# Reordering the convolution chunks of a hybrid diffusion backbone: vector taps, sigmoid products and modulation matmuls

## The chip, the core and the metric

The kernel runs on one core of a Trainium2 chip. TensorE (PE in the rows) multiplies matrices into PSUM; VectorE (DVE), ScalarE (ACT) and GpSimd (POOL) work element by element; SyncE (SP) issues the transfers, which run on the core's 16 DMA engines. Each engine works through its own queue in order, and semaphores hold an instruction until what it reads is there and what it writes is free. The metric is the device time of one execution in microseconds, as the median of several runs.

## The reference, cut to what matters

Two layers run over 1024 latent and 256 context tokens of width 1024. The change lies in the first layer's Conformer convolution module, a gated linear unit followed by a depthwise convolution of 31 taps, a LayerNorm and a second matmul; and in the modulation vectors, a small matmul of SiLU(c) with a large weight matrix.

```python
sc = jax.nn.silu(c)
mod_lat = (sc @ ada_w[i] + ada_b[i])[:, None, :]
sh1, sc1, g1, sh2, sc2, g2 = jnp.split(mod_lat, 6, axis=-1)

def conformer_conv(h, w_pw1, b_pw1, w_dw, b_dw, ln_g, ln_b, w_pw2, b_pw2):
    u = h @ w_pw1 + b_pw1
    a, g = jnp.split(u, 2, axis=-1)
    v = a * jax.nn.sigmoid(g)
    v = dwconv(v, w_dw, b_dw)          # 31 taps per channel
    v = jax.nn.silu(layernorm(v, ln_g, ln_b))
    return v @ w_pw2 + b_pw2
```

## The kernel before

Channels lie on the 128 partitions, tokens along the free dimension, in three token tiles: 0 and 1 with 512 latent tokens each, 2 with the 256 context tokens. The convolution stage goes over eight chunks c of 128 channels. It is a software pipeline: the loop body for c convolves chunk c while the matmuls of the gated linear unit for chunk c + 1 run (`q` is that next chunk, `q.v` its gated result). All four compute engines have their order written out by hand here: inside `tc.manual_schedule` an instruction stands on its engine's queue where the program names it. SP's queue alone is ordered by the scheduler.

The pieces of the body, with their lines:

- `glu_mm(q, t, half)` (L193): one half, gate (0) or value (1), of token tile t, three groups of eight matmuls, since every product of full precision is made of a high and a low part (`wh`, `wl`, `xh`, `xl`). The results alternate between two PSUM banks (`glu_ps`).
- `glu_gate` (L746, ScalarE) takes the sigmoid of the gate half; `glu_mul` (L751, VectorE) multiplies it with the value half into `v`. `vp.load` (L799, L792) writes a part of `v` to DRAM and reads it back shifted by one token per tap (`vp`, `vpb`), for TensorE.
- The 31 taps of chunk c are divided. Eight go to TensorE in chunks 0 to 5 (16 in chunk 6, 28 in chunk 7): `taps` (L822), small diagonal matmuls into the one PSUM accumulator `cacc`. `NDV`, 13 taps (8 in chunk 6, none in chunk 7), go to VectorE: `dq` (L843), each of which adds one tap into `cacc`, so they start when TensorE is done with it. The rest are made as products on ScalarE (`first`, L838, and `pq`, L848, `pr`, two buffers) and added by GpSimd (L849) in a second accumulator `a`.
- `last()` (L853): three VectorE adds join `cacc` and `a` to `y`. They free `cacc` for the next chunk's matmuls. `ymean` (L862) accumulates the mean of y on TensorE.
- `ada` (L211): the modulation of block 4 + c, eight matmuls in four parts, each of which reads one 512 KB weight tile `raw`. Then comes a copy out of PSUM (L217, ScalarE) and, in the next chunk as `fin`, a transpose and bias (L223, L226, L231). `ld_ada` (L109) issues the load of a part.
- `w_load`, `w_hi` (L914, ScalarE) and `w_lo` (L919, VectorE, `wl`): load and split of the next two weight tiles of the gated linear unit.

All weight tiles go through the same two `raw` buffers, in the order: modulation parts 0 and 1, parts 2 and 3, two weight tiles. A load therefore waits until the tile two places ahead has been read. `run(steps, n)` takes the next n steps of a list:

```python
pq = [lambda j=j: prod(j)() for j in range(npe + ndve + 1, TAPS)]
dq = [lambda j=j: dve(j) for j in range(npe, npe + ndve)]
return [lambda: part(0), lambda: part(1), lambda: part(2), lambda: part(3), evac, finish]
```

Chunk 7 has no next gated linear unit; its body is the `else` branch. There `load_ada` (L878) loads 2 MB modulation weights of the second layer into the input tiles that are no longer needed. Behind the loop come the LayerNorm and the second matmul.

Of the kernel before, what the change touches and what calls it, by code (L numbers as in the profile page):

```python
# [52 lines left out]
def hybrid_dit_kernel(  # L53
# [555 lines left out]
    with ExitStack() as cs:  # L609
# [255 lines left out]
        def run(steps, n):  # L865
            for _ in range(min(n, len(steps))):
                steps.pop(0)()
# [54 lines left out]
        with tc.manual_schedule(engines=CONV_ENGINES):  # L922
# [16 lines left out]
            q = glu_begin(0)  # L939
# [36 lines left out]
            wh = w_hi()  # L976
# [11 lines left out]
            for c in range(KC):  # L988
                wide_taps = M[c] * P > 256
                if wide_taps:  # L990
                    dgs = tap_weights(c)
                r, taps = pe_taps(c, vp, dgs)
                first, pq, dq, last = conv_steps(c, q.v, r, NPE[c], NDV[c])
                ada_ps = pc.tile([P, 512], F32, tag="s", name="ada_ps", bufs=2) if c == KC - 1 else None
                ada = ada_steps(0, 4 + c, lambda u, c=c: araw[c, u], ada_ps)
                if c + 1 < KC:
                    q = glu_begin(c + 1)
                    glu_mm(q, 0, 0)
                    glu_gate(q, 0)
                    glu_mm(q, 0, 1)  # L1000
                    glu_mul(q, 0)
                    if fin:
                        fin()
                    run(taps, 4)
                    run(ada, 2)
                    ld_ada(c, 2)
                    ld_ada(c, 3)
                    first()
                    run(pq, 2)
                    vp = Shifted(c + 1, q.v)  # L1010
                    vp.load(0)
                    if c > 0:
                        ymean(c - 1)
                    glu_mm(q, 1, 0)
                    run(pq, 2)
                    glu_gate(q, 1)
                    run(ada, 2)
                    w_load()
                    w_load()
                    run(dq, 3)  # L1020
                    glu_mm(q, 1, 1)
                    run(ada, 1)
                    run(dq, 3)
                    glu_mul(q, 1)
                    vp.load(1)
                    run(pq, 1)
                    if M[c + 1] * P <= 256:
                        dgs = tap_weights(c + 1)
                    wh = w_hi()
                    glu_mm(q, 2, 0)  # L1030
                    run(dq, 1)
                    w_lo(wh)
                    ld_ada(c + 1, 0)
                    run(pq, 1)
                    glu_gate(q, 2)
                    wh = w_hi()
                    glu_mm(q, 2, 1)
                    run(dq, 1)
                    glu_mul(q, 2)
                    vp.load(2)  # L1040
                    w_lo(wh)
                    ld_ada(c + 1, 1)
                    run(pq, 99)
                    run(dq, 99)
                    fin = ada.pop()
                else:
                    run(ada, 2)
                    ld_ada(c, 2)
                    ld_ada(c, 3)
                    fin()  # L1050
                    first()
                    run(pq, 99)
                    ymean(c - 1)
                    run(taps, 2)
                    run(ada, 3)
                    for i in range(4):
                        load_ada(i)
                    run(taps, 2)
                    run(dq, 99)
                last()  # L1060
        cvs.close()
# [771 lines left out]
```

## Time and profile before

| what | value |
|---|---|
| median of 3 runs | 2767.87 us (2767.05 to 2770.55) |
| the profiled execution | 2768.97 us, its span 2767.2 us |
| TensorE busy over the span | 2646.0 us (96%) |
| VectorE, ScalarE, GpSimd busy | 1622.0, 984.5, 549.5 us |
| mean granted TensorE clock | 0.986 of full speed |
| convolution stage, first to last convolution matmul | 91.6 to about 403 us |

The page's shares are averages over stages with different limits. The stage that the change touches is some 310 us of the 2767. Start and end times below are microseconds from the span's start. "Idle before" is the time for which the engine had nothing to do ahead of a row, with the event that ended it; "issue" there means that the profile shows no event for it.

### The profile page before, as it was taken

How to read it: one execution, taken by the hardware profiler on the slowest of the kernel's cores; microseconds unless marked ns; L12 is line 12 of the kernel's file. 1: busy time of each engine (PE TensorE's matmuls, PEld its weight loads, DVE VectorE, ACT ScalarE, POOL GpSimd, SP SyncE). 2: the span in 40 equal slices, each digit the busy share in tenths (PEclk: the TensorE clock that was granted, in tenths of full speed). 3: DMA queues.
4: the chain of work that ended last, by engine and by line, in shares of the span. 5: the costliest groups of instructions: out<-in, count | busy, mean ns of one | idle time of the engine just before them, and what ended most of it. 6: DMA issues, size and time to landing. Idle time of an engine off the chain costs nothing.

```text
span 2767.2 us, 34117 instructions
## 1 busy us (share of the span) xinstructions
PE 2646.0 (96%) x13860; PEld 2145.8 (78%) x13860; DVE 1622.0 (59%) x2273; ACT 984.5 (36%) x1396; POOL 549.5 (20%) x384
## 2 busy tenths in 40 slices
PE   5999978999999999999999999999999999999997
PEld 3676644778888888888888787788878888888886
DVE  6576635454454544444546757999865545555546
ACT  6444425552211122211123426777652222222223
POOL 1576623230000000000002204566420000000003
PEclk8999999999999999999999999999999999999998
DMA  6554665322111111111111451331111111111111
GB/s 243 163 172 152 203 212 196 109 84 69 39 39 39 38 39 39 39 39 38 37 40 37 152 190 45 73 81 52 39 54 48 52 46 49 51 46 46 53 47 69
DMA packets 81774, 225.38 MB, mean 81 GB/s; under 512 B 10832, under 2 KB 22736, under 8 KB 79312
## 3 DMA queue, kind: packets, MB, share of 16 engines
q1 hardware_dynamic: 81616, 223.20, 24.5%
q8 instruction: 109, 1.79, 0.3%
q14 instruction: 49, 0.40, 0.0%
HBM read 202.00 MB, written 21.16 MB: 81 GB/s over the span
## 4 chain that ended last, share of the span: by engine, by line
PE 78%; DVE 10%; ACT 5%; DMA 3%; issue 2%; POOL 1%; SPq 1%; DVEq 0%; ACTq 0%; POOLq 0%
PE up_ps L193 38%; PE dn_ps L193 18%; PE glu_ps L193 4%; PE wo_ps L193 3%; PE cacc L822 2%; PE pw_ps L193 2%; DVE cacc L843 2%; PE pB L193 2%; DMA raw<-in_adaw_dram 2%; PE pA L193 2%; PE tp L1544 1%; DVE tl L178 1%; PE v_ps L193 1%; PE ada_ps L211 1%; DVE mx L1522 1%
## 5 line engine op out<-in xcount | busy, mean ns | idle before, releaser
L131 DVE TENSOR_TENSOR wl<-raw,wh 128x1024 fp32r<-128x1024 f32 x165 | 204.8, 1242 | 514.7 <-issue 311.1
L193 PE MATMUL up_ps<-x_l,wh 128*128 128x512 f32 (+1 forms) x1760 | 413.8, 369 | 4.2 <-POOL x_l L322 4.2
L193 PE MATMUL up_ps<-x_h,wl 128*128 128x512 f32 (+1 forms) x1760 | 408.7, 368 | 0.2 <-ACT x_h L311 0.2
L193 PE MATMUL up_ps<-x_h,wh 128*128 128x512 f32 (+1 forms) x1760 | 406.9, 368 | 0.0
L193 PEld LDWEIGHTS up_ps<-x_l,wh 128*128 128x128 f32 x1760 | 311.2, 188 | 64.0 <-POOL x_l L322 5.8
L193 PEld LDWEIGHTS up_ps<-x_h,wh 128*128 128x128 f32 x1760 | 310.7, 189 | 55.6 <-issue 0.8
L193 PEld LDWEIGHTS up_ps<-x_h,wl 128*128 128x128 f32 x1760 | 309.9, 189 | 56.0 <-issue 0.8
L257 POOL TENSOR_TENSOR acc<-acc,scrh 128x256 f32<-128x256 f32 (+1 forms) x36 | 37.5, 1041 | 1574.1 <-ACT scrh L256 1572.3
L461 DVE SCALAR_TENSOR_TENSOR y<-dn_ps,mods,y 128x512 f32<-128x512 f32 (+1 forms) x400 | 270.3, 694 | 129.2 <-PE dn_ps L193 129.1
L416 ACT ACTIVATE c<-up_ps,pv 128x1282 f32<-128x1282 f32 (+1 forms) x88 | 115.7, 1316 | 586.8 <-PE up_ps L193 586.8
L129 ACT CAST wh<-raw 128x1024 fp32r<-128x1024 f32 x178 | 185.5, 1043 | 357.7 <-PE dn_ps L193 328.1
L193 PE MATMUL dn_ps<-gl,wh 128*128 128x512 f32 (+1 forms) x800 | 233.0, 372 | 0.7 <-DVE y L461 0.7
L193 PE MATMUL dn_ps<-gh,wl 128*128 128x512 f32 (+1 forms) x800 | 231.5, 371 | 0.0
L193 PE MATMUL dn_ps<-gh,wh 128*128 128x512 f32 (+1 forms) x800 | 231.1, 370 | 0.0
L849 POOL TENSOR_TENSOR a<-a,pr 128x1295 f32<-128x1295 f32 x62 | 190.2, 3068 | 95.8 <-ACT pr L848 93.3
L1538 POOL TENSOR_TENSOR p<-p,rd 128x640 f32<-128x640 f32 (+1 forms) x128 | 154.7, 1240 | 233.0 <-DVE rd L1536 164.5
L420 DVE SCALAR_TENSOR_TENSOR c<-up_ps,pv,c 128x1281 f32<-128x1281 f32 (+1 forms) x88 | 124.6, 1416 | 121.2 <-ACT c L416 121.2
L193 PEld LDWEIGHTS dn_ps<-gl,wh 128*128 128x128 f32 x800 | 142.7, 188 | 31.8 <-DVE y L461 6.4
L193 PEld LDWEIGHTS dn_ps<-gh,wh 128*128 128x128 f32 x800 | 145.1, 188 | 27.0
L193 PEld LDWEIGHTS dn_ps<-gh,wl 128*128 128x128 f32 x800 | 145.1, 188 | 27.0
L843 DVE SCALAR_TENSOR_TENSOR cacc<-v,pv,cacc 128x1295 f32<-128x1295 f32 x86 | 134.9, 1569 | 43.8 <-PE cacc L822 41.7
L424 DVE SCALAR_TENSOR_TENSOR c<-up_ps,pv,c 128x1281 f32<-128x1281 f32 (+1 forms) x88 | 124.5, 1416 | 2.3
(255 smaller groups left out, 4029.0 us busy)
## 6 DMA issues: line engine op xcount, KB each, us to landing
raw<-in_up_dram SPq DMA_DIRECT2D x88, 512.0 KB, 3.4
ada<-in_adaw_dram SPq DMA_DIRECT2D x11, 2048.0 KB, 9.2
raw<-in_down_dram SPq DMA_DIRECT2D x44, 512.0 KB, 3.4
raw<-in_adaw_dram SPq DMA_DIRECT2D x38, 512.0 KB, 4.9
raw<-in_pw_dram SPq DMA_DIRECT2D x32, 512.0 KB, 3.5
vpb<-v_dram SPq DMA_DIRECT2D x32, 256.0 KB, 4.5
qs<-q_dram SPq DMA_DIRECT2D x32, 256.0 KB, 5.9
raw<-in_wo_dram SPq DMA_DIRECT2D x16, 512.0 KB, 3.5
```

The lines of the kernel that those rows point to most:

```text
L129: nc.scalar.copy(out=wh, in_=raw)
L131: lo_engine[0].tensor_sub(out=wl, in0=raw, in1=wh)
L193: nc.tensor.matmul(ps, lhsT=w, rhs=x, start=first and n == 0, stop=last and n == len(seq) - 1)
L257: (eng or nc.gpsimd).tensor_add(out=acc, in0=acc, in1=sq)
L416: nc.scalar.activation(out=c, in_=ps[:, :W], func=AF.Identity, bias=seg("fdb", l * 2 * NJ + ab * NJ + j, 1), scale=wd[1])
L420: nc.vector.scalar_tensor_tensor(out=c[:, 1:W], in0=ps[:, 0:W - 1], scalar=wd[0], in1=c[:, 1:W], op0=ALU.mult, op1=ALU.add)
L424: nc.vector.scalar_tensor_tensor(out=c[:, 0:W - 1], in0=ps[:, 1:W], scalar=wd[2], in1=c[:, 0:W - 1], op0=ALU.mult, op1=ALU.add)
L461: nc.vector.scalar_tensor_tensor(out=h, in0=ps[:, m * n:(m + 1) * n], scalar=mod(l, 5, dc, s), in1=h, op0=ALU.mult, op1=ALU.add)
L822: nc.tensor.matmul(r["acc"][32 * g:32 * g + 32, o:e], lhsT=w[:, (4 * s + g) * 32:(4 * s + g + 1) * 32], rhs=vp.rows(g, s, o, e - o), start ...
L843: nc.vector.scalar_tensor_tensor(out=acc, in0=v[:, j:j + OW], scalar=tap(j), in1=acc, op0=ALU.mult, op1=ALU.add)
L849: return lambda: nc.gpsimd.tensor_tensor(out=r["a2"], in0=r["a2"], in1=pr, op=ALU.add)
L1538: nc.gpsimd.tensor_tensor(out=it.p4[:, hh, :it.wid], in0=it.p4[:, hh, :it.wid], in1=rd[:, hh:hh + 1].to_broadcast([P, it.wid]), op=ALU.mult)
```

## The change

Only the order of calls in the loop body changes. In chunks 0 to 6 parts 0 and 1 of the modulation stand ahead of the convolution matmuls, instead of behind them, and parts 2 and 3 behind `ymean`, instead of between two groups of the gated linear unit. Five products instead of four stand ahead of the second token tile's sigmoid, and a sixth directly behind it. Nine vector taps (all eight in chunk 6) stand ahead of the second token tile's gate product, where six were and a seventh and eighth between later steps. In chunk 7 parts 0 and 1 come behind the first half of the convolution matmuls instead of ahead of the previous chunk's `fin`.

```diff
--- before.py
+++ after.py
@@ -999,34 +999,34 @@
                     glu_gate(q, 0)
                     glu_mm(q, 0, 1)
                     glu_mul(q, 0)
+                    run(ada, 2)
+                    ld_ada(c, 2)
+                    ld_ada(c, 3)
                     if fin:
                         fin()
                     run(taps, 4)
-                    run(ada, 2)
-                    ld_ada(c, 2)
-                    ld_ada(c, 3)
                     first()
-                    run(pq, 2)
+                    run(pq, 3)
                     vp = Shifted(c + 1, q.v)
                     vp.load(0)
                     if c > 0:
                         ymean(c - 1)
-                    glu_mm(q, 1, 0)
-                    run(pq, 2)
-                    glu_gate(q, 1)
                     run(ada, 2)
                     w_load()
                     w_load()
-                    run(dq, 3)
+                    glu_mm(q, 1, 0)
+                    run(ada, 1)
+                    run(pq, 2)
+                    glu_gate(q, 1)
+                    run(pq, 1)
                     glu_mm(q, 1, 1)
-                    run(ada, 1)
-                    run(dq, 3)
+                    run(dq, 9)
                     glu_mul(q, 1)
                     vp.load(1)
+                    wh = w_hi()
                     run(pq, 1)
                     if M[c + 1] * P <= 256:
                         dgs = tap_weights(c + 1)
-                    wh = w_hi()
                     glu_mm(q, 2, 0)
                     run(dq, 1)
                     w_lo(wh)
@@ -1044,18 +1044,18 @@
                     run(dq, 99)
                     fin = ada.pop()
                 else:
-                    run(ada, 2)
-                    ld_ada(c, 2)
-                    ld_ada(c, 3)
                     fin()
                     first()
                     run(pq, 99)
                     ymean(c - 1)
                     run(taps, 2)
+                    run(ada, 2)
+                    ld_ada(c, 2)
+                    ld_ada(c, 3)
+                    run(taps, 2)
                     run(ada, 3)
                     for i in range(4):
                         load_ada(i)
-                    run(taps, 2)
                     run(dq, 99)
                 last()
         cvs.close()
```

VectorE, from the convolution of chunk 1 to the end of its y (`cacc` are the taps, `v<-glu_ps` the gate products, `wl` the weight splits), before:

```order
L843 SCALAR_TENSOR_TENSOR cacc<-v,pv,cacc 128x1295 x6
L751 SCALAR_TENSOR_TENSOR v<-glu_ps,pv,sg 128x512
L843 SCALAR_TENSOR_TENSOR cacc<-v,pv,cacc 128x1295
L919 TENSOR_TENSOR wl<-raw,wh 128x1024
L843 SCALAR_TENSOR_TENSOR cacc<-v,pv,cacc 128x1295
L751 SCALAR_TENSOR_TENSOR v<-glu_ps,pv,sg 128x256
L919 TENSOR_TENSOR wl<-raw,wh 128x1024
L843 SCALAR_TENSOR_TENSOR cacc<-v,pv,cacc 128x1295 x5
L853 TENSOR_TENSOR y_677<-cacc,a_1085 128x512
```

and with the change, in the same place:

```order
L843 SCALAR_TENSOR_TENSOR cacc<-v,pv,cacc 128x1295 x9
L751 SCALAR_TENSOR_TENSOR v<-glu_ps,pv,sg 128x512
L843 SCALAR_TENSOR_TENSOR cacc<-v,pv,cacc 128x1295
L919 TENSOR_TENSOR wl<-raw,wh 128x1024
L843 SCALAR_TENSOR_TENSOR cacc<-v,pv,cacc 128x1295
L751 SCALAR_TENSOR_TENSOR v<-glu_ps,pv,sg 128x256
L919 TENSOR_TENSOR wl<-raw,wh 128x1024
L843 SCALAR_TENSOR_TENSOR cacc<-v,pv,cacc 128x1295 x2
L853 TENSOR_TENSOR y_677<-cacc,a_1085 128x512
```

Three taps went from behind the second split to ahead of the first gate product; the total stays 13.

TensorE from the transpose of the previous modulation block (`ada_pt`) over the convolution matmuls of chunk 1 (`ada_ps` are modulation parts, `xl_470` an input of token tile 1), before:

```order
L223 MATMUL ada_pt<-ident,ada_sb 128x128 x4
L822 MATMUL cacc<-vp,dg 32x512 x8
L822 MATMUL cacc<-vp,dg 32x272 x8
L822 MATMUL cacc<-vpb,dg 32x240 x8
L822 MATMUL cacc<-vpb,dg 32x271 x8
L211 MATMUL ada_ps<-raw,c_80 32x512 x4
L862 MATMUL ymean<-y_677,ones_88 32x512
L862 MATMUL ymean<-y_678,ones_88 32x512
L862 MATMUL ymean<-y_679,ones_88 32x256
L193 MATMUL glu_ps<-xl_470,wh 128x512 x8
```

and with the change:

```order
L211 MATMUL ada_ps<-raw,c_80 32x512 x4
L223 MATMUL ada_pt<-ident,ada_sb 128x128 x4
L822 MATMUL cacc<-vp,dg 32x512 x8
L822 MATMUL cacc<-vp,dg 32x272 x8
L822 MATMUL cacc<-vpb,dg 32x240 x8
L822 MATMUL cacc<-vpb,dg 32x271 x8
L862 MATMUL ymean<-y_677,ones_88 32x512
L862 MATMUL ymean<-y_678,ones_88 32x512
L862 MATMUL ymean<-y_679,ones_88 32x256
L211 MATMUL ada_ps<-raw,c_80 32x512 x4
```

Parts 0 and 1 went from behind the convolution to ahead of it. The row at the end of the second piece is parts 2 and 3, which stood three groups of `glu_ps` further on before.

SP's queue from the write of the first part of a chunk's `v` to the write of its second, before:

```order
L799 DMA v_dram_1093<-v 128x527
L792 DMA vp<-v_dram_1093 128x1x512 x4
L109 DMA raw<-in_adaw_dram 128x1024 x2
L109 DMA raw<-in_pw_dram 128x1024 x2
L799 DMA v_dram_1093<-v 128x527
```

and with the change:

```order
L799 DMA v_dram_1096<-v 128x527
L109 DMA raw<-in_adaw_dram 128x1024 x2
L792 DMA vp<-v_dram_1096 128x1x512 x4
L109 DMA raw<-in_pw_dram 128x1024 x2
L799 DMA v_dram_1096<-v 128x527
```

The loads of modulation parts 2 and 3 changed places with the four shifted copies. Near the end of the loop one 2 MB load (L878) moved too: from behind the last pair of modulation loads to directly ahead of the four shorter `vp` copies for chunk 7.

## Rows read from the trace of the kernel before

**Rows 1.** Chain that ended last, in time; columns: start us, us, what.
```profile
199.40 3.54 DVE wl L919
...
211.12 1.56 issue
```
**Rows 2.** Windows of one chunk: PE, PEld, DVE, ACT, POOL busy; clock, DMA, GB/s.
```profile
239.40:280.50 41.10, 38.27 (x236) 27.32 (x236) 29.09 (x24) 17.70 (x17) 28.45 (x13) 0.96 0.50 159
```
**Rows 3.** Waits, 91.6 to 336.6 us: engine, line, released by; total us, times, longest.
```profile
PE cacc L822 <- issue: 12.2, 5, 2.5
```
**Rows 4.** Timeline of TensorE, one chunk; start us, us, instruction, [idle before].
```profile
212.68 4.54 PE L822 MATMUL cacc<-vp,dg 128*32 128x512 f32 x32 [2.44 <-issue]
...
218.73 1.07 PE L211 MATMUL ada_ps<-raw,c 128*32 128x512 f32 x8
...
220.58 2.11 PE L193 MATMUL glu_ps<-xl,wh 128*128 128x512 f32 x8
...
226.70 1.05 PE L211 MATMUL ada_ps<-raw,c 128*32 128x512 f32 x4 [0.39 <-DMA raw<-in_adaw_dram]
...
228.95 2.11 PE L193 MATMUL glu_ps<-xl,wh 128*128 128x512 f32 x8
...
234.54 1.11 PE L193 MATMUL glu_ps<-xh,wl 128*128 128x256 f32 x8
...
240.29 2.00 PE L193 MATMUL glu_ps<-xl,wh 128*128 128x512 f32 x8
...
251.21 0.60 PE L223 MATMUL ada_pt<-ident,ada_sb 128*128 128x128 f32 x4
254.25 4.34 PE L822 MATMUL cacc<-vp,dg 128*32 128x512 f32 x32 [2.45 <-issue]
```
**Rows 5.** Timeline of TensorE, starts of the convolution in chunks 0 and 6.
```profile
91.62 2.84 PE L822 MATMUL cacc<-vp,dg 128*32 128x512 f32 x32
...
96.00 1.04 PE L211 MATMUL ada_ps<-raw,c 128*32 128x512 f32 x8
...
336.65 8.45 PE L822 MATMUL cacc<-vp,dg 128*32 128x512 f32 x64 [2.96 <-DVE y L853]
```
**Rows 6.** Windows of the convolution matmuls: PE, PEld, DVE; clock, DMA share, GB/s.
```profile
92.60:93.60 1.00, 1.00 (x17) 0.30 (x13) 0.00 (x0) 1.00 0.23 86
213.60:214.60 1.00, 1.00 (x8) 0.27 (x4) 0.00 (x0) 0.50 0.45 179
```
**Rows 7.** Timeline of VectorE: chunk 0's second split, then chunks 2 and 3.
```profile
81.29 1.22 DVE L919 TENSOR_TENSOR wl<-raw,wh 128x1024 fp32r<-128x1024 f32 x1
...
210.96 1.62 DVE L853 TENSOR_TENSOR y<-cacc,a 128x512 f32<-128x512 f32 x3
...
219.00 9.61 DVE L843 SCALAR_TENSOR_TENSOR cacc<-v,pv,cacc 128x1295 f32<-128x1295 f32 x6 [5.46 <-PE cacc L822]
234.81 0.75 DVE L751 SCALAR_TENSOR_TENSOR v<-glu_ps,pv,sg 128x512 f32<-128x512 f32 x1 [6.20 <-PE glu_ps L193]
```
**Rows 8.** Timeline of GpSimd, the first adds of chunk 3.
```profile
215.54 12.15 POOL L849 TENSOR_TENSOR a<-a,pr 128x1295 f32<-128x1295 f32 x4 [4.43 <-ACT pr L848]
```
**Rows 9.** DMA issues near 203, 220 and 375.6 us: KB each, us to landing.
```profile
raw<-in_adaw_dram SPq DMA_DIRECT2D x1, 512.0 KB, 4.5
...
raw<-in_adaw_dram SPq DMA_DIRECT2D x2, 512.0 KB, 7.1
...
ada<-in_adaw_dram SPq DMA_DIRECT2D x1, 2048.0 KB, 12.0
```
**Rows 10.** Timelines at the last chunk: VectorE, TensorE and SP.
```profile
371.28 1.61 DVE L853 TENSOR_TENSOR y<-cacc,a 128x512 f32<-128x512 f32 x3
...
381.24 1.92 PE L211 MATMUL ada_ps<-raw,c 128*32 128x512 f32 x4 [9.08 <-DMA raw<-in_adaw_dram]
...
384.18 1.06 PE L822 MATMUL cacc<-vp,dg 128*32 128x512 f32 x1
...
367.05 0.33 SPq L109 DMA_DIRECT2D raw<-in_adaw_dram  x1
```

## The prediction

> **What bounds the kernel now.** I read the page first: TensorE is busy for 96% of the span, so only a stage in which it still waits can give time, and the change touches one stage, the convolution, from about 91 to 403 us. The chain in order of time shows how that stage runs [rows 1]: a weight split, then vector taps (the 1.56 us of "issue" at 211.12 is the vector engine's three adds that finish y), then the convolution matmuls. So at each chunk's start the chain lies on VectorE, not on TensorE. The windows confirm that no engine is full over a chunk [rows 2]: in 41.10 us TensorE is busy 38.27, VectorE 29.09, GpSimd 28.45. The list of waits prices it [rows 3]: before the convolution matmuls TensorE stood still 12.2 us in 5 chunks (the row says "issue", but y ends at 210.96 + 1.62 = 212.58 [rows 7] and the matmuls start at 212.68 [rows 4]: that is the release).
>
> Why is y late? VectorE gets the sums at 219.00, does six taps in 9.61 us (1.60 each), and then stands 6.20 us in front of the gate product, which is written ahead of the other seven taps and needs a matmul that ends at 234.8 [rows 7]. Those idle microseconds come back as the wait at the next chunk.
>
> The wait costs twice. After the 2.45 us the granted clock is 0.50, the 1.2 GHz level; in chunk 0, where nothing was waited for, it is 1.00 [rows 6]. From the first convolution matmul to the first modulation matmul it took 218.73 - 212.68 = 6.05 us in chunk 3, and 96.00 - 91.62 = 4.38 in chunk 0 [rows 4, 5]: 1.67 us for the clock.
>
> **The change, part by part.**
>
> *Nine taps ahead of the gate product.* Nothing is added; 3 taps per chunk, 4.8 us, move into the 6.20 us of idle time. In the new order VectorE, from the end of the convolution matmuls, has 13 taps x 1.60 = 20.8, gate products 0.7 + 0.45, y 1.6 and two weight splits. A split took 3.54 us beside GpSimd's adds [rows 1] and 1.22 with GpSimd idle [rows 7]. So the vector work is 26.0 to 30.7 us if nothing makes it wait.
>
> The Trainium skill has a rule that speaks against the change here: by the GPSIMD Engine Reference, section 8 (Key points), GpSimd shares its SBUF interfaces with VectorE and disturbs vector instructions with two SBUF inputs. The trace agrees (3.54 against 1.22 for the split, while a tap, with one input in PSUM, kept its 1.60 beside GpSimd's adds). By that rule the products that are moved forward bring GpSimd's adds beside the first split too, and the vector work is 30.7 us; without it 26.0.
>
> *The new chunk on TensorE.* The wait goes if VectorE is done before TensorE comes round. TensorE's period is then the old one less its losses. From 212.68 to 254.25 it was 41.57 us [rows 4]. Off it: the wait 2.45; the clock 1.67; and the interruption by modulation parts 2 and 3. Between the end of the first gate matmuls and 228.95 these took 0.39 of idle time + (228.95 - 226.70) = 2.64 us [rows 4], against 0.9 for the same eight matmuls in one go (parts 0 and 1 and then ymean take 220.58 - 218.73 = 1.85 together [rows 4], ymean's three matmuls about half): 1.7 less. New period 41.57 - 2.45 - 1.67 - 1.7 = 35.75 us. VectorE has 35.75 - 4.4 = 31.3 us for its 26.0 to 30.7: hidden, with 0.6 to 5.3 to spare. If that cover goes, each missing microsecond shows once, and again at the low clock.
>
> *Who waits for the gate product now.* It comes 4.4 + 9 x 1.60 = 18.8 us after the chunk's start and ends at 19.5. Its bank is needed by the second matmul group of the short token tile: 4.4 + 1.85 + two groups of 5.6 + one of 2.9 = 20.3. Hidden, by 0.8.
>
> *Products ahead of the sigmoid.* GpSimd's loop runs from y: accumulator start and first product on ScalarE 1.4 each, nine adds of 3.04 [rows 8] = 27.3, tap weights 0.6, y 1.6: 32.3 us, under 35.75. The five products ahead of the sigmoid end about 12 us into the chunk, when the sigmoid's input is just ready. No cost.
>
> *Modulation parts moved.* Parts 0 and 1 go ahead of the convolution matmuls, 2 and 3 behind ymean. On SP's queue the loads for 2 and 3 now stand ahead of the four vp copies, which wait for the convolution's end. They are free to go once parts 0 and 1 have read their buffers, 1.5 us before the convolution starts, and are needed 4.4 + 1.0 after that: 6.9 us later. One load alone lands in 4.5 us, a pair beside the vp copies in 7.1 [rows 9]. I take the former, since the copies now come behind, and allow 0.3 per chunk. The load for part 1 is released by the second split. It ends at 18.8 + 0.7 + 1.6 + 3.54 + 1.6 + 0.45 + 3.54 = 30.2 us into the chunk at worst (25.6 with both splits at 1.22); part 1 starts when the next tile's two groups and part 0 are through, 4.4 + 1.85 + 11.2 + 5.75 + 10.9 + 0.45 = 34.55 [rows 4]. That leaves 4.3 to 8.9 us for a landing of 4.5: hidden but for 0.2 at worst, which the allowance covers.
>
> *Sum over chunks.* Six periods from 91.62 to 336.65 took 245.0 [rows 5]. New: 6 x (35.75 + 0.3) = 216.3, and 0.9 for parts 0 and 1 ahead of chunk 0's convolution: **27.8 us saved**. The ends are 29.6 (no allowance used) and 18 (27.8 less 6 x 1.67, if the low clock stayed).
>
> *The last two chunks.* Chunk 6 has twice the convolution matmuls; its first 64 took 8.45 us at the low clock where chunk 0's 32 took 2.84 [rows 5]: 2 x 2.84 = 5.7, so 2.8 is saved. In chunk 7 TensorE waited 9.08 us for one modulation load and began the convolution at 384.18 [rows 10]; the change puts that part behind the first half of the convolution. What is late next is y of chunk 6, done at 371.28 + 1.61 = 372.9 [rows 10], and the shifted copies vp. With y and its mean alone the start moves up by 384.2 - 372.9 - 1.0 = 10.3. But a 2 MB load now stands directly ahead of the vp copies, and such a load took 12.0 us to land [rows 9]: leaving right behind the load that went at 367.05 [rows 10] by the old run's clock, it holds them until 379 or so, and the gain is 4. I take the middle, 7. Parts 2 and 3 and the copy out of PSUM now follow the convolution: 0.9 + 0.6 = 1.5 back. End: 2.8 + 7 - 1.5 = **8.3 us saved** (5.3 to 11.6).
>
> Total 27.8 + 8.3 = 36.1. The profiled execution took 2768.97 us (span 2767.2): 2732.9, say **2733 us**. The median of the runs, 2767.87, lies 1.1 lower, within the rounding.
>
> **The rivals.**
> 1. *The late modulation load takes the place of the y wait.* If landings are 7.1 us as in the pair of today and both splits cost 3.54, part 1 comes 7.1 - 4.3 = 2.8 late a chunk, right ahead of the convolution, and the low clock returns its 1.67. 4.5 x 6 = 27 back, less the 1.8 allowed: 2758; with the splits halfway (2.4 us each) 0.5 late and hardly a low clock, 2736. For it: the queue is busy with v and vpb there. Against: today's load at that place landed in 4.5. Chance 0.14.
> 2. *The clock gain does not come*, since some other short wait (y by a few tenths, part 2) keeps opening at the convolution. 6 x 1.67 = 10 lost: 2743. Chance 0.12.
> 3. *The next stage gives it back.* The LayerNorm stage needs 2 MB modulation loads; if they, and not TensorE, set its start, the last chunks' 8 and part of the rest are lost. With 12 us per load [rows 9] and two of them: 24 back, 2757. Against: two of the four are issued over 30 us before use. Chance 0.06.
> 4. *VectorE becomes the bound: slower than before.* Now 13 taps must fit between two convolutions. Today's average period is 40.8; it is exceeded when 13t + 9.9 + 4.4 > 40.8, from t = 2.04 us per tap. If the nine taps in a row beside GpSimd slowed as the split does (3.54/1.22 = 2.9 times), t is 4.6, the period 4.4 + 60.3 + 9.9 = 74.6 and the time 2769 + 6 x 34 = 2973. Against: six taps at 1.60 ran beside four adds of GpSimd [rows 7, 8]. Chance 0.03.
>
> **How the numbers follow.** Forecast 0.65, for 2725 to 2743: the lower end is no allowance (1.8), 3.3 more at the end and 3 for row rounding over six chunks. The range goes up to rival 1's middle and beyond, to 2755, and leaves out its worst end, rival 3, rival 4 and what lies below: 2725 to 2755. A measurement here tells 0.2%, 5.5 us, from no change: all of the forecast, rivals 1 and 2 and most of 3 are faster by more. Faster 0.93, same 0.04, slower 0.03.
>
> **What would show it.** In the changed profile: convolution matmuls 35.7 to 36.4 us apart in chunks 1 to 6, each with clock 1.00 and some 4.4 us long; "issue" ahead of them gone from the waits; VectorE's nine taps in one stretch of 14.4 us with the gate product directly behind, y done 0.5 to 3 us before the convolution; part 1 without a DMA wait over 0.5; chunk 7's convolution about 37 us behind chunk 6's, not 47.5. I am wrong if the period stays over 38 us, if TensorE waits for raw ahead of the convolution, or if the time saved by 403 us is not found at the end.

## The result, and the profile after

| | median | ratio to before, 95% interval |
|---|---|---|
| before, beside it | 2769.11 us (2767.05 to 2770.55, 4 runs) | |
| changed | 2738.15 us (2737.24 to 2741.94, 4 runs) | 0.9891 [0.9874, 0.9908] |

The change saves 31 us where 36 was forecast (2733, range 2725 to 2755). The profiled execution took 2738.22 us, its span 2736.4. One later execution of the changed kernel took 4459.85 us, at a mean granted clock of 0.598 instead of 0.99, and is left out of every ratio.

One chunk of the changed kernel in the windows view (columns as in [rows 2]); the second row is a microsecond within its convolution matmuls, and answers to the 0.50 in [rows 6]:

```profile
204.50:240.60 36.10, 36.10 (x235) 26.85 (x234) 28.58 (x23) 17.44 (x16) 29.48 (x14) 1.00 0.58 180
205.00:206.00 1.00, 1.00 (x16) 0.32 (x12) 0.87 (x1) 0.12 (x1) 0.92 (x2) 1.00 1.20 269
```

TensorE is now busy for all of the 36.10 us, and the convolution runs at the full clock. The list of TensorE's waits from 92.8 to 313.4 us (chunks 0 to 5, as in [rows 3]) has one line left, and y is not in it:

```profile
PE ada_ps L211 <- DMA raw<-in_adaw_dram: 2.7, 3, 1.6
```

TensorE's timeline follows: first the same chunk, 3, to be read beside [rows 4]; then chunk 0, which takes longer than the others; then the last two chunks.

```profile
202.90 1.07 PE L211 MATMUL ada_ps<-raw,c 128*32 128x512 f32 x8
203.89 0.66 PE L223 MATMUL ada_pt<-ident,ada_sb 128*128 128x128 f32 x4
204.48 2.84 PE L822 MATMUL cacc<-vp,dg 128*32 128x512 f32 x32
...
208.86 1.03 PE L862 MATMUL ymean<-y,ones 128*32 128x512 f32 x6
209.72 1.60 PE L211 MATMUL ada_ps<-raw,c 128*32 128x512 f32 x8
211.25 2.11 PE L193 MATMUL glu_ps<-xl,wh 128*128 128x512 f32 x8
...
240.60 2.84 PE L822 MATMUL cacc<-vp,dg 128*32 128x512 f32 x32
...
92.87 2.82 PE L822 MATMUL cacc<-vp,dg 128*32 128x512 f32 x32
...
98.36 1.05 PE L211 MATMUL ada_ps<-raw,c 128*32 128x512 f32 x4 [0.94 <-DMA raw<-in_adaw_dram]
101.00 1.92 PE L211 MATMUL ada_ps<-raw,c 128*32 128x512 f32 x4 [1.59 <-DMA raw<-in_adaw_dram]
...
313.46 5.49 PE L822 MATMUL cacc<-vp,dg 128*32 128x512 f32 x64
...
343.36 1.64 PE L862 MATMUL ymean<-y,ones 128*32 128x512 f32 x6 [1.94 <-DVE y L853]
349.66 11.35 PE L822 MATMUL cacc<-vp,dg 128*32 128x512 f32 x107 [4.66 <-DMA vp<-v_dram]
```

And VectorE in the same chunk, beside [rows 7]:

```profile
209.12 14.43 DVE L843 SCALAR_TENSOR_TENSOR cacc<-v,pv,cacc 128x1295 f32<-128x1295 f32 x9 [3.24 <-PE cacc L822]
223.45 0.74 DVE L751 SCALAR_TENSOR_TENSOR v<-glu_ps,pv,sg 128x512 f32<-128x512 f32 x1
...
225.59 1.22 DVE L919 TENSOR_TENSOR wl<-raw,wh 128x1024 fp32r<-128x1024 f32 x1
...
228.69 2.61 DVE L919 TENSOR_TENSOR wl<-raw,wh 128x1024 fp32r<-128x1024 f32 x1
...
234.50 1.62 DVE L853 TENSOR_TENSOR y<-cacc,a 128x512 f32<-128x512 f32 x3
```

The nine taps run in one piece, the gate product follows with no idle time, and y is done at 236.12, 4.48 us before the convolution that needs its accumulator. The forecast had 0.5 to 3 us there, with longer splits. Before, the same engine stood 6.20 us ahead of the gate product, and TensorE waited for y [rows 3, 7].

The next table shows where the 30.8 us between the two spans lie. It is worked out from the starts of the convolution in chunks 0 to 7: 92.87, 132.79, 168.80, 204.48, 240.60, 276.65, 313.46, 349.66 in the changed kernel, and 91.62, 131.43, 171.50, 212.68, 254.25, 295.32, 336.65, 384.18 before.

| stretch | before | after | saved |
|---|---|---|---|
| start to chunk 0's convolution | 91.62 | 92.87 | -1.25 |
| chunk 0's to chunk 6's convolution | 245.03 | 220.59 | 24.44 |
| chunk 6's to chunk 7's convolution | 47.53 | 36.20 | 11.33 |
| chunk 7's convolution to the LayerNorm's first wait for a square (`yvar`) | 31.33 | 33.05 | -1.72 |
| from there to the end of the span | 2351.69 | 2353.69 | -2.00 |

The code of the last stretch is the same in both.

### The profile page after: what moved, and what is told of

Its sections match the earlier page's. It is cut to its first block, busy times and chain, and to the rows that moved or that the text cites. A ratio compares the mean times of both kernels' runs of the same rounds, so it can differ in the third digit from the quotient of the medians.

```text
span 2736.4 us, 34110 instructions
## 1 busy us (share of the span) xinstructions
PE 2635.3 (96%) x13860; PEld 2150.8 (79%) x13860; DVE 1617.1 (59%) x2273; ACT 982.9 (36%) x1396; POOL 555.3 (20%) x384
## 4 chain that ended last, share of the span: by engine, by line
PE 81%; DVE 9%; ACT 6%; DMA 2%; issue 2%; POOL 1%; SPq 0%; DVEq 0%; ACTq 0%; POOLq 0%
PE up_ps L193 39%; PE dn_ps L193 18%; PE glu_ps L193 7%; PE wo_ps L193 2%; PE pw_ps L193 2%; PE pB L193 2%; PE pA L193 2%; PE cacc L822 2%; DVE tl L178 1%; PE tp L1544 1%; PE v_ps L193 1%; DVE mx L1522 1%; PE ada_ps L211 1%; ACT p L1526 1%; PE dn_tail L193 1%
```

## The experiments

The change has four parts: the nine taps, the products (with the weight cast that changes places with them), the modulation passes in chunks 0 to 6, and the last chunk. Four kernels make one part of it alone, and three leave out one part or two. One tests the clock, and three, beside a second measurement of the changed kernel, try to get the forecast's missing microseconds. The table has all runs. "Conv 0 to 6" is the time from the start of chunk 0's convolution to that of chunk 6's, "conv 6 to 7" the time from there to chunk 7's, and "rest" what follows the wait at `yvar`. These three columns come from one profiled execution of each kernel; the medians come from all its executions.

| kernel | median, us | ratio to before, 95% | conv 0 to 6, us | conv 6 to 7, us | rest, us |
|---|---|---|---|---|---|
| before | 2769 to 2770 | | 245.0 | 47.5 | 2351.7 |
| taps alone | 2753.15 | 0.9943 [0.9928, 0.9958] | 227.4 | 44.2 | 2356.8 |
| modulation alone | 2747.78 | 0.9925 [0.9910, 0.9940] | 224.6 | 41.9 | 2356.4 |
| products alone | 2759.42 | 0.9965 [0.9953, 0.9977] | 234.8 | 44.5 | 2354.4 |
| last chunk alone | 2758.75 | 0.9965 [0.9951, 0.9980] | 240.6 | 35.8 | 2353.9 |
| taps and products | 2748.64 | 0.9925 [0.9902, 0.9949] | 221.8 | 44.8 | 2356.9 |
| all but the taps | 2740.18 | 0.9894 [0.9874, 0.9914] | 220.8 | 36.0 | 2356.0 |
| all but the products | 2741.87 | 0.9902 [0.9881, 0.9923] | 223.7 | 35.3 | 2352.1 |
| before, TensorE kept busy | 2766.26 | 0.9984 [0.9972, 0.9995] | 238.5 | 44.2 | 2352.6 |
| changed, again | 2740.41 | 0.9894 [0.9875, 0.9913] | 221.4 | 35.4 | 2355.1 |
| chunk 0 later | 2736.80 | 0.9879 [0.9863, 0.9896] | 218.1 | 35.2 | 2355.1 |
| 2 MB loads later | 2735.57 | 0.9879 [0.9861, 0.9897] | 220.4 | 30.9 | 2352.9 |
| both of these | 2734.33 | 0.9873 [0.9855, 0.9891] | 219.0 | 30.9 | 2355.2 |

### Each part alone

**Taps alone:**

```diff
-                    run(dq, 3)
                     glu_mm(q, 1, 1)
                     run(ada, 1)
-                    run(dq, 3)
+                    run(dq, 9)
                     glu_mul(q, 1)
```

> Only the nine vector taps go ahead of the second tile's gate product; products and modulation stay where they were. Theory (the wait for y and the low clock that follows it make most of the gain): the waits of 5 x 2.45 + 2.96 us and the low clock of 5 x 1.67 + 2.8 us go, some 26 us, to about 2743 us (2739 to 2750); convolution starts 36 to 37.5 us apart, its 64 matmuls 4.4 us long, clock 1.00. Rival (the modulation loads make the gain): at most a few microseconds, 2762 or more.

Measured 2753.15, 10 us over what the theory gave and above its range. TensorE's wait for y did fall, to 0.4 us (0.57 in chunk 6), and the clock stayed full. But y now waited for another engine. These are VectorE ahead of chunk 5's convolution, and GpSimd in the same stretch:

```profile
273.52 3.17 DVE L843 SCALAR_TENSOR_TENSOR cacc<-v,pv,cacc 128x1295 f32<-128x1295 f32 x2
279.56 1.62 DVE L853 TENSOR_TENSOR y<-cacc,a 128x512 f32<-128x512 f32 x3 [2.87 <-POOL v L730]
```

```profile
260.13 3.02 POOL L849 TENSOR_TENSOR a<-a,pr 128x1295 f32<-128x1295 f32 x1 [2.56 <-ACT pr L848]
...
263.67 3.00 POOL L849 TENSOR_TENSOR a<-a,pr 128x1295 f32<-128x1295 f32 x1
269.51 10.01 POOL L849 TENSOR_TENSOR a<-a,pr 128x1295 f32<-128x1295 f32 x3 [2.83 <-ACT pr L848]
```

VectorE is through with its taps at 276.7 and waits 2.87 us for GpSimd, whose last adds end at 279.52. (The row names L730, which clears the margins of the next `v` directly behind those adds.) GpSimd had stood still twice for products that ScalarE had queued in its old order: 2.56 us behind the modulation's copy out of PSUM, and 2.83 us behind a sigmoid and a weight cast. So the period, the time from one convolution to the next, stays at 37.0 to 38.7 us, bound by GpSimd.

**Modulation alone** (parts 0 and 1 ahead of `fin()` and the convolution, 2 and 3 and the weight loads behind `ymean`, the copy out of PSUM behind the first gate group; the last chunk as before):

```diff
                     glu_mul(q, 0)
+                    run(ada, 2)
+                    ld_ada(c, 2)
+                    ld_ada(c, 3)
                     if fin:
                         fin()
                     run(taps, 4)
-                    run(ada, 2)
...
                         ymean(c - 1)
+                    run(ada, 2)
+                    w_load()
+                    w_load()
                     glu_mm(q, 1, 0)
+                    run(ada, 1)
                     run(pq, 2)
                     glu_gate(q, 1)
-                    run(ada, 2)
```

> Only the modulation parts move in chunks 0 to 6. Theory: VectorE still does seven taps behind the gate product, so y is still last; the path from the convolution over the gate matmuls and 19.3 us of vector work to y is 38.4 us a chunk instead of 41.1, chunk 0 loses some 2 us, net about 11 saved, 2758 us (2751 to 2765), with a wait for y at the convolution still in the profile. Rival (the modulation loads make the gain): 25 or more saved, 2744 or less.

Measured 2747.78: better than the expectation's whole range, and the best part alone. TensorE at two convolutions, and VectorE ahead of the gate product between them:

```profile
205.50 2.84 PE L822 MATMUL cacc<-vp,dg 128*32 128x512 f32 x32 [1.32 <-issue]
...
242.46 2.85 PE L822 MATMUL cacc<-vp,dg 128*32 128x512 f32 x32 [1.31 <-issue]
```

```profile
210.13 9.61 DVE L843 SCALAR_TENSOR_TENSOR cacc<-v,pv,cacc 128x1295 f32<-128x1295 f32 x6 [3.77 <-PE cacc L822]
223.01 0.75 DVE L751 SCALAR_TENSOR_TENSOR v<-glu_ps,pv,sg 128x512 f32<-128x512 f32 x1 [3.27 <-PE glu_ps L193]
```

With the modulation out of its way TensorE delivers the gate product's input sooner, so VectorE stands there for 3.27 us instead of 6.20 [rows 7]. That alone halves the wait for y, from 2.45 to 1.3 us, and after 1.3 us the clock did not fall. So one move shrinks three losses: the interruption, the wait and the clock.

**Products alone:**

```diff
                     first()
-                    run(pq, 2)
+                    run(pq, 3)
...
                     glu_gate(q, 1)
+                    run(pq, 1)
...
                     vp.load(1)
+                    wh = w_hi()
                     run(pq, 1)
...
-                    wh = w_hi()
```

> Only the products move ahead of the sigmoid. Theory and rivals alike: ScalarE and GpSimd are not on the path, no change, 2769 us (2766 to 2772). If GpSimd's accumulator were what y waits for, 5 or more would be saved.

Measured 2759.42, where no effect was expected: a miss. The wait for y became uneven, 0.5 to 3.4 us, and the low clock followed only one of the six waits:

```profile
207.71 2.84 PE L822 MATMUL cacc<-vp,dg 128*32 128x512 f32 x32 [3.35 <-issue]
247.35 4.39 PE L822 MATMUL cacc<-vp,dg 128*32 128x512 f32 x32 [3.10 <-issue]
```

The traces show what sets the time here. GpSimd, in chunk 3, and VectorE's first split in chunks 3 and 4:

```profile
210.57 21.45 POOL L849 TENSOR_TENSOR a<-a,pr 128x1295 f32<-128x1295 f32 x7 [4.43 <-ACT pr L848]
```

```profile
229.39 3.70 DVE L919 TENSOR_TENSOR wl<-raw,wh 128x1024 fp32r<-128x1024 f32 x1
...
270.48 2.24 DVE L919 TENSOR_TENSOR wl<-raw,wh 128x1024 fp32r<-128x1024 f32 x1
```

With the products made earlier GpSimd adds seven of them without a pause, and the first split ends 1.1 us behind the last of these adds, early or late as it may have begun: 233.09 against 232.02 in chunk 3, and 272.72 against 271.6 in chunk 4. In chunks 1 and 2 the distance is the same, and these four chunks all take 39.6 us, chunk 4 with its low clock too. So by these rows the path to y leads over GpSimd's adds and the splits, and what TensorE does not lose to the clock, it spends waiting.

**Last chunk alone:**

```diff
                 else:
-                    run(ada, 2)
-                    ld_ada(c, 2)
-                    ld_ada(c, 3)
                     fin()
...
                     run(taps, 2)
+                    run(ada, 2)
+                    ld_ada(c, 2)
+                    ld_ada(c, 3)
+                    run(taps, 2)
                     run(ada, 3)
```

> Only chunk 7's order changes (its modulation parts behind the halves of the convolution). Theory: the 9.08 us wait for a modulation load ahead of chunk 7's convolution goes and the start is set by y or by the shifted copies: 6 to 10 saved, 2761 us (2758 to 2764). Rival (the transfer is as late for the copies as for the modulation part): under 3 saved, 2766 or more.

Measured 2758.75, as expected: conv 6 to 7 takes 35.8 us instead of 47.5. Chunks 0 to 6 are not edited here, and the wait for y is as before to 0.02 us. All the same the convolution ran at the full clock in two of chunks 1 to 5 (2.84 us, where it took 4.3 to 4.5 before), so part of the 4.4 us by which conv 0 to 6 is shorter in this profile is chance:

```profile
171.69 2.84 PE L822 MATMUL cacc<-vp,dg 128*32 128x512 f32 x32 [2.44 <-issue]
210.26 2.84 PE L822 MATMUL cacc<-vp,dg 128*32 128x512 f32 x32 [2.46 <-issue]
249.34 4.48 PE L822 MATMUL cacc<-vp,dg 128*32 128x512 f32 x32 [2.45 <-issue]
```

The four parts alone save 0.57, 0.75, 0.35 and 0.35%, 2.0% in sum; together they save 1.1%. They remove the same idle time from several sides. TensorE's rows show it. Before, its six waits ahead of the convolution in chunks 1 to 6 are 15.2 us, and the first 32 matmuls of each convolution in chunks 1 to 5 take 22.0 us in sum at the low clock, where the changed kernel's take 14.2. The taps alone leave 2.6 us of the waits, the modulation alone 8.3, the products alone 11.4; the 22.0 us fall to 14.2, 14.2 and 15.8. Added up, the three take 23.3 us off waits of 15.2, and 21.9 off a loss of 7.8.

### One part left out

**All but the taps** (the changed kernel with `run(dq, 3)` on either side of `glu_mm(q, 1, 1)` instead of `run(dq, 9)`):

> The changed kernel with six taps ahead of the gate product again (all else as changed). My theory: the nine taps are what lets y be done early; without them the wait for y comes back as in the run with the modulation move alone (1.3 to 1.7 us a chunk there, conv 37 us apart). Period 37, conv at full clock mostly; chunk 7 as in the changed kernel: 2738 + 6 x 1 = 2744 us (2740 to 2749). Rival, the taps are worth nothing beside the other two parts: period 36, under 2739.

Measured 2740.18, as good as the changed kernel's second measurement, 2740.41. The time lies at the lower edge of my range and does not decide; the profile does. Conv 0 to 6 takes 220.8 us against 220.6 and 221.4 in the two profiles of the changed kernel. VectorE and TensorE in chunk 3:

```profile
224.34 0.75 DVE L751 SCALAR_TENSOR_TENSOR v<-glu_ps,pv,sg 128x512 f32<-128x512 f32 x1 [3.25 <-ACT wh L914]
...
226.48 2.73 DVE L919 TENSOR_TENSOR wl<-raw,wh 128x1024 fp32r<-128x1024 f32 x1
...
231.00 2.15 DVE L919 TENSOR_TENSOR wl<-raw,wh 128x1024 fp32r<-128x1024 f32 x1
```

```profile
206.85 2.84 PE L822 MATMUL cacc<-vp,dg 128*32 128x512 f32 x32 [0.19 <-issue]
```

The idle time ahead of the gate product is there (3.25 us), yet TensorE waits for y by 0.2 us at most in chunks 1 to 5: the gate product starts as late in the chunk as with the modulation alone (17.5 us), but the two splits behind it take 4.9 us here and 5.8 there (3.18 and 2.60). That the moved products, by placing GpSimd's adds elsewhere, make the splits shorter is likely, but no run tests it by itself. The rival was right: beside the other parts the nine taps save nothing that can be measured. What they buy is slack, 4.48 us between y and the convolution instead of none.

**All but the products:**

> The changed kernel with the products of tiles 0 and 1 in their old places on ScalarE (four ahead of the sigmoid, the first product of the last tile behind the gate product, the weight casts after it). My theory: with taps done early, GpSimd's adds are the last thing that y waits for, as in the run with the taps alone (VectorE waited 2.87 us for v there): VectorE's y add is ended by POOL again, period 36.8 to 37.8, 2738 + 6 x 1.3 = 2746 us (2741 to 2751). Rival, my blind prediction's sentence that the move of the products has no effect of its own: 2738 (2736 to 2740).

Measured 2741.87, between the two. The mechanism of my theory was there. VectorE ahead of chunk 4's convolution:

```profile
239.75 1.62 DVE L853 TENSOR_TENSOR y<-cacc,a 128x512 f32<-128x512 f32 x3 [2.87 <-POOL v L730]
```

But y ends at 241.37 and the convolution starts at 242.15, so the wait is hidden, by 0.8 us. The period is 36.5 to 37.9 us in chunks 1 to 5, conv 0 to 6 some 2.7 us longer than in the two profiles of the changed kernel, and part of that is TensorE's wait for modulation loads (4.3 us in 7 waits against 2.7 in 3). In the medians the difference lies within the intervals.

**Taps and products**, with the modulation and the last chunk in their old places:

> The kernel before with the nine taps and the products moved, but the modulation passes and the last chunk in their old places. My theory: y is no longer waited for and the clock stays full, and what is left of the old period is the interruption by parts 2 and 3 (1.7 us) and their late loads: period 37 to 38, chunk 7 begins 10 us late as before: 2738 + 6 x 1.5 + 6 = 2753 us (2747 to 2758). Rival, the modulation move was not needed in chunks 1 to 6: period 36, only the last chunk's part missing: 2744.

Measured 2748.64, within the range, with the period a little shorter, 36.3 to 36.9 us in chunks 1 to 4. No wait for y is left. Parts 2 and 3 still interrupt the gate matmuls, from 215.06 to 217.26:

```profile
216.28 1.05 PE L211 MATMUL ada_ps<-raw,c 128*32 128x512 f32 x4 [0.17 <-DMA raw<-in_adaw_dram]
217.26 2.11 PE L193 MATMUL glu_ps<-xl,wh 128*128 128x512 f32 x8
```

That is 2.20 us instead of the 2.64 of [rows 4], so by the forecast's reckoning the interruption costs 1.3 us here and not 1.7. What the move is worth beside the taps and the products is less still: the periods of chunks 1 to 4 are 0.2 to 0.9 us longer here than in the changed kernel, and chunk 0's, 37.19, is 2.7 us shorter. So conv 0 to 6 is only 1.2 us longer without the part that saved most alone.

### Does the wait bring the low clock?

This is the kernel before, with the transposes that precede the convolution repeated, so that TensorE works where it stood:

```diff
-            for m in range(4):
+            for m in [m for _ in range(pe_again[0]) for m in range(4)]:
                 nc.tensor.transpose(out=pt[:, m * P:(m + 1) * P], in_=r["sb"][:, m * P:(m + 1) * P],
...
+                        pe_again[0] = 5
                         fin()
+                        pe_again[0] = 1
```

> The kernel before, with the four transposes of each modulation part's end repeated four more times ahead of the convolution, so that TensorE works through most of the wait for y instead of standing still. The wait itself stays (y ends when it did). Theory, the low clock comes from standing still: the convolution's 32 matmuls take 2.8 us instead of 5.3, granted clock 1.00, some 1.7 us a chunk back: 2769 - 6 x 1.7 = 2759 us (2754 to 2764). Rival, the low clock is not the wait's doing: the convolution stays at 5.3 us in most chunks and the time at 2767 or over. If the transposes run past y they cost up to 1 us a chunk: then 2765.

TensorE's timeline ahead of chunk 3:

```profile
209.44 2.35 PE L225 MATMUL ada_pt<-ident,ada_sb 128*128 128x128 f32 x20
212.48 2.84 PE L824 MATMUL cacc<-vp,dg 128*32 128x512 f32 x32 [0.69 <-issue]
```

The idle time is 0.7 us instead of 2.45, and in chunks 1 to 6 every convolution runs at the full clock (2.84 us for 32 matmuls, where the rows of before have 4.29 to 4.54 and not the 5.3 of the expectation; 5.49 for the 64 of chunk 6). Conv 0 to 6 is 6.6 us shorter, though TensorE still goes on only when y is done (212.38). With 2.45 us of idle time two of ten convolutions in chunks 1 to 5 kept the full clock (none of five before, two of five with the last chunk alone); with 0.7 us five of five did. So in these profiles standing still brings the low clock, but not every time.

In the time the theory is met only in part. The profiled execution took 2760.29 us, as it wanted, but that is the fastest of ten; their median is 2766.26, 4 us less than before where 10 were expected. No other execution's trace is there, so it stays open whether the clock fell in the slower ones all the same, or whether they lost time elsewhere.

### Towards the forecast's missing microseconds

**Changed, again:**

> The changed kernel once more, on the chip on which the three below run, so that they have something to be compared with. 2738 us (2736 to 2741); conv of chunk 0 and 1 some 40 us apart again, chunk 7's conv 36 us behind chunk 6's with a wait of some 4 us for vp.

Measured 2740.41 us. The same two places wait, 1.61 us for a modulation load in chunk 0 and 3.85 us for vp in chunk 7.

**Chunk 0 later:**

```diff
+                    if c == 0:
+                        glu_mm(q, 1, 0)
                     run(ada, 2)
                     w_load()
                     w_load()
-                    glu_mm(q, 1, 0)
+                    if c > 0:
+                        glu_mm(q, 1, 0)
```

> The changed kernel, but in chunk 0 alone, where no mean of an earlier chunk stands between, modulation parts 2 and 3 (and the two weight loads that follow) come one matmul group later, behind the first gate group of tile 1. Theory: chunk 0's 39.92 us against 36 elsewhere come from the loads of parts 2 and 3, which land 6.0 us after their issue while TensorE is there after 4.7, and from the low clock behind that wait; with 5.7 us more they have landed: chunk 0's period 36.5 to 37.5, the later ones as before, 2738 - 3 = 2735 us (2733 to 2738). Rival, the long first period is the start-up of the pipeline (vp, weights) and not the loads: 40 us again and 2738 or over.

Chunk 0's period went from 39.92 to 36.98, with the pair of parts in one row and no wait ahead of it:

```profile
101.75 1.98 PE L193 MATMUL glu_ps<-xh,wh 128*128 128x512 f32 x8
103.66 1.06 PE L211 MATMUL ada_ps<-raw,c 128*32 128x512 f32 x8
...
130.50 2.84 PE L822 MATMUL cacc<-vp,dg 128*32 128x512 f32 x32
```

That is 2.9 us, as expected, so the loads cause 2.9 of the 3.9 us by which chunk 0 exceeds the others; the last one stays open. The median is 2736.80, 1.4 to 3.6 us below the changed kernel's two, but the executions overlap (2734.30 to 2738.65 here), so in the time the gain is likely and not shown.

**2 MB loads later** (a one-column write by VectorE into the two buffers makes their loads wait until chunk 6's y is done; `load_ada` is called ahead of `fin()`):

```diff
             w = p_.tile([P, KC, 512], F32, tag=tag, name=f"ada1_{i}", bufs=1)
+            if i in (2, 3):
+                nc.vector.memset(w[:, 0, 0:1], 0.0)
...
                 else:
+                    for i in range(4):
+                        load_ada(i)
                     fin()
```

> The changed kernel, but the two 2 MB modulation loads of the last chunk that have no earlier buffer to wait for are held back until chunk 6's y is done, so that the copies vp of chunk 7 leave ahead of them. Theory: vp took 6.5 us to land because a 2 MB load was under way; with it behind, vp lands in 2.6 to 4 us, the wait of 4.66 us ahead of chunk 7's matmuls falls to 0.5 to 2, and 2738 - 3.5 = 2734.5 us (2732 to 2738). Rival, the held loads land late for the next stage, which uses them some 30 us later (a 2 MB load took 12.0 us, two of them 24): the gain is gone again by the LayerNorm's variance and the time stays at 2738 or goes to 2741.

The transfers between 336 and 356 us (KB each, us to landing), and TensorE:

```profile
vp<-v_dram SPq DMA_DIRECT2D x4, 144.5 KB, 3.8
```

```profile
343.46 0.59 PE L822 MATMUL cacc<-vp,dg 128*32 128x512 f32 x1
...
362.76 3.17 PE L211 MATMUL ada_ps<-raw,c 128*32 128x512 f32 x8 [2.56 <-DMA raw<-in_adaw_dram]
```

The copies vp land in 3.8 instead of 6.5 us, the wait of 4.66 is gone, and the convolution of chunk 7 starts 5.3 us sooner after chunk 6's. So the 2 MB load did hold vp up. But only 2.3 us of the gain are left at `yvar`: the loads of parts 2 and 3 now go out behind the two 2 MB loads, TensorE waits 2.56 us for them, and the eight matmuls behind the wait take 3.17 us instead of 1.07, at a granted clock of 0.50. The rival was right that a late load gives part of the gain back, though not about which load. The median is 2735.57, with the same caveat: the executions (2734.20 to 2741.26) overlap with those of the changed kernel.

**Both:**

> The changed kernel with both edits above. If the two waits are independent, their gains add: 2738 - 3 - 3.5 = 2731.5 us (2728 to 2736). If one of them moves the stage so that the other returns: 2734 to 2738. Either way the later stages vary by 2 to 5 us with short waits and the low clock behind them, which could hide half of it.

Measured 2734.33 us. Three of its four executions (2732.39, 2732.56, 2736.10, 2738.62) are faster than all eight of the changed kernel (2737.24 to 2741.94). The intervals of the ratios to before overlap, so that it beats the changed kernel is likely and not shown. In its profiled execution, the slowest of the four, the two gains did not add: chunk 1 took 37.56 us, chunk 7's wait for the modulation load grew to 3.10, and `yvar` comes at 381.65 against the changed kernel's 382.71.

## Why the prediction was right, and where it was off

**The bound.** Right: at each chunk's start TensorE waited for VectorE, and with that wait gone TensorE is busy for 36.10 of 36.10 us.

**The period, 35.75 + 0.3.** Right for chunks 1 to 4: 36.01, 35.68, 36.12 and 36.05. The nine taps took 14.43 us, and the gate product ended 19.7 us into the chunk (19.5 forecast).

**Who earns it.** The step "The wait goes if VectorE is done before TensorE comes round" gave the y wait and its clock to the taps, and to the modulation only its interruption. The runs show otherwise: of the 24.4 us from conv 0 to conv 6 the taps alone give 17.6, the modulation alone 20.5, the products alone 10.2, and any two of them 21.3 to 24.3. The three terms were right as a sum, since that sum is TensorE's work without a wait, whichever edit takes the wait away. They were not separable, since y's lateness hangs on TensorE's own delay ahead of the gate product. That the total came out does not bear out the shares that it gave to the parts.

**"Products ahead of the sigmoid ... No cost."** As far as it goes, right. But I compared GpSimd's sum of 32.3 us with the period, and not its end with the moment when y needs it. With the taps early and the old order on ScalarE, GpSimd releases y 2.87 us after VectorE has asked. And alone the move saves 10 us, where I had put its gain at nothing.

**The allowance for late loads, 0.3 us a chunk.** This is the term that was mis-sized. It holds in chunks 1 to 4, where the pair of loads lands in 4.6 to 5.1 us. It is used there: in chunk 3 the weight loads (PEld) of parts 2 and 3 stand 0.7 us for `raw`, which the list of PE's own waits does not show, and the eight matmuls take 1.53 us (209.72 to 211.25) where the sum had 0.9. In chunk 0 the pair lands in 6.0 us, and "needed 4.4 + 1.0 after that" is wrong there: chunk 0 has no `ymean`, which is the 1.0. It took 39.92 us, 3.9 too many; chunk 5 (5.7 us to landing) took 36.81, 0.8 too many. With 0.35 us more lost at the start (1.25 against 0.9) and 0.3 won in chunks 1 to 4 that is the 4.6 between the 27.8 forecast and the 23.2 measured at conv 6.

**The last two chunks, 8.3.** The clock of chunk 6 gives 2.96 us (2.8 forecast; 5.49 us for the 8.45 of [rows 5]). Chunk 7 starts 8.4 us sooner (7 forecast, between 4 and 10.3). Before, two modulation parts stood ahead of it with their waits, the second in [rows 10], the first here:

```profile
371.10 1.05 PE L211 MATMUL ada_ps<-raw,c 128*32 128x512 f32 x4 [2.76 <-DMA raw<-in_adaw_dram]
```

That is 2.76 + 1.05 + 9.08 + 1.92 = 14.8 us. In their place TensorE now waits 1.94 us for y and 4.66 us for vp, which a 2 MB load holds up as the forecast's lower end had it, only for less time; the difference is 8.2 of the 8.4. Behind, 1.72 us are lost (1.5 forecast): 9.6 saved in all.

**"If the time saved by 403 us is not found at the end".** 2 us of it are not. At the start of the feed-forward stage, whose code is the same, TensorE waits 1.50 us in the changed kernel and 1.52 before; after the one the clock fell, after the other it didn't. TensorE's timeline of the changed kernel:

```profile
556.91 0.38 PE L399 MATMUL up_ps<-c,ident 128*128 128x2 f32 x2 [1.50 <-ACT ada_sb L217]
...
559.07 1.05 PE L223 MATMUL ada_pt<-ident,ada_sb 128*128 128x128 f32 x4
```

Its windows view has a clock of 0.50 there:

```profile
559.00:561.00 2.00, 2.00 (x8) 1.74 (x7) 0.53 (x3) 1.04 (x1) 0.00 (x0) 0.50 0.64 233
```

and before:

```profile
589.93 0.38 PE L399 MATMUL up_ps<-c,ident 128*128 128x2 f32 x2 [1.52 <-ACT ada_sb L217]
...
591.65 0.60 PE L223 MATMUL ada_pt<-ident,ada_sb 128*128 128x128 f32 x4
```

Of the 2.0 us, 1.6 go here: from 557.15 to the first `mean_ps` matmul at 562.05 it is 4.90 us, and before, from 590.18 to 593.48, it is 3.30. No part of the change goes with it: all fourteen profiles have a wait of 1.50 to 1.52 us here, and the same stretch takes 4.86 to 4.92 us in eight of them and 3.29 to 3.30 in six. The six are before, the last chunk alone, all but the products, TensorE kept busy, 2 MB loads later, and both late edits. Over the fourteen the whole stretch behind `yvar`, which no kernel edits, takes 2351.7 to 2356.9 us, and before has the shortest. So 1.6 us of the miss look like chance; what decides in which execution the clock falls stays open.

**The rivals.** None came true in the profile: VectorE did not become the bound (1.60 us a tap in a row of nine), the clock gain came in every chunk from 1 to 6, no wait for a load stood ahead of the convolution in chunks 1 to 6, and no wait for the next stage's loads shows up to `yvar`.

**The rule on shared SBUF interfaces** (the Trainium skill, GPSIMD Engine Reference, section 8, Key points) agrees with the trace: splits took 1.21 to 3.96 us over these runs, by how much of GpSimd's work lay beside them, while the taps kept their 1.60. It goes the other way too: at 225.59 the split kept its 1.22, and GpSimd's tap weights, made beside it, took 1.69 us instead of some 0.6. In the changed kernel the lengthened splits are hidden; with the products alone they lie on the path to y.

## What to carry to other kernels

When an engine waits at a ring of dependences (here TensorE, VectorE, GpSimd and back to TensorE each chunk), add up the saving at the ring, not per edit. Up to chunk 6 any two of three edits gave 87 to 99% of it, so each one was nearly dispensable, the one that looked like the cause too. For each edit ask what comes second to last at the same place, at that moment and not over the period: with y it was GpSimd, 2.87 us behind VectorE. And price the time that a load has for its landing in each iteration, the first and the last ones above all, since what gives it time elsewhere may be missing there.

## What was not expected of the hardware

The same wait does not always cost the clock. Ahead of the convolution a wait of 2.44 to 2.46 us was followed by the full clock in two of five chunks of the run with the last chunk alone, one of 3.35 us by the full clock with the products alone, and one of 3.10 us in the same run by 4.39 us for what takes 2.84 otherwise. After 1.3 to 1.7 us it did not fall in any of the six convolutions with the modulation alone; after 1.50 to 1.52 us at the feed-forward stage it fell in eight of fourteen profiles. A gain that rests on the clock, like the 1.67 us a chunk of the prediction, is thus an amount that one execution may get and another not. The ten executions of the kernel in which TensorE was kept busy lie 10 us apart (2760.29 to 2770.36); whether the clock makes that spread is not shown.
